# Wider steps between the blocks of the up operands, the projection weights and the out-projection weights in SBUF

## The chip, the cores and the metric

The kernel runs on one core of one Trainium2 chip. The metric is the device time of one execution in microseconds (us), lower being better. The kernel before takes 1240.32 us, the median of three runs (1239.75 to 1241.23).

## The reference

One decoder layer on x of 1024 tokens by 1024 features, in float32:

```
h    = rms_norm(x, norm1_w)
proj = h @ w_in                        # 1024 x 3592
A    = differential attention of 4 heads over proj's first 1536 columns
B    = gated DeltaNet of 4 heads: causal conv + SiLU of the next 1536 columns (q, k, v),
       chunked delta rule; gated by silu(z), z and two small gates being the last 520 columns
x    = x + concat(A, B) @ w_out        # 1024 x 1024
h    = rms_norm(x, norm2_w)
out  = x + square(relu(h @ w_up)) @ w_down   # hidden 4096
```

## The kernel before

Every large product works on float32 numbers that are split in two float32r parts. ScalarE (ACT) rounds a block to a high part, VectorE (DVE) subtracts it from the block and so writes the low part. A product then takes three matmuls for each block of 128 of the summed dimension: high by high, high by low and low by high. The normed and transposed activations lie as such pairs in hH and hL: eight blocks (k) of 1024 columns for each partition, so that one block starts 4096 bytes behind the one before. Each matmul has a stationary operand of 128 columns (512 bytes a partition), loaded by an instruction of its own (PEld), and a moving operand of 256, 260 or 512 columns that streams through.

The stages, in order of time:

1. **Gates (z)**, to 58 us. `z_mm` (L370 to L381) multiplies hH and hL (stationary) by two units of 260 weight columns (moving). Each unit has eight blocks of 260 columns, laid one behind the other: 1040 bytes from block to block.
2. **DeltaNet projections (ps_dn)**, 58 to 230 us. `load_unit` (L183) fetches 256 columns of weights and rounds them in steps of two blocks (L192 on ACT, L193 on DVE); `trn` (L275) makes a block of the weights the stationary operand, and 512 columns of hH or hL the moving one. Interleaved are the transposes, convolutions and triangular inverses of the delta rule.
3. **Attention projections (ps_qk)**, 230 to 460 us. `da_units` (L1037) makes hH and hL stationary and 256 columns of weights moving (L1063 to L1065). The weights come by `Quarters.unit` (L253) and its roundings (L224, L225). An interleaving planner (`Interleave`) puts the steps of the scan over chunks, of the attention scores and of the values between the matmuls.
4. **Out-projection (ps_op)**, 460 to 620 us. `half` (L1325) has hH and hL stationary and 512 columns of w_out moving (L1332 to L1334), four blocks a unit, again from `Quarters.unit`. Attention's last scores and values and the second norm stand between them.
5. **Up**, 620 to 928 us. `prod_up` (L1503) makes 128 columns of an up operand stationary and 512 tokens of hH and hL, or of sums of them (T0 to T2), moving. An operand is a high and a low tile `op` of four blocks by 256 columns, rounded by `split` (L1425, L1426) from `operand` (L1604), or by `rounded` and `rest` (L1630, L1634). The tiles rotate through five buffers. The first 96 of these matmuls (`up_first`) take other tiles.
6. **Down**, from 928 us. `down` (L1789) takes both operands from views of hH and hL.

In the built program the starts of hH, hL, both wH, both wL, T0 to T2 and all five op buffers have the same remainder, 320, when divided by 512. Blocks of the weights with 256 columns start 1024 bytes apart, those with 512 columns 2048, and those of op 1024: the remainder stays the same from block to block. In the gates alone it moves by 16 bytes a block.

TensorE's order in stages 3 to 6 is written out (`manual_schedule`); a scheduler orders what the source leaves open. The functions that the change touches:

Of the kernel before, what the change touches and what calls it, by code (L numbers as in the profile page):

```python
# [10 lines left out]
F32R = mybir.dt.float32r  # L11
# [7 lines left out]
P = 128  # L19
SEQ = 1024  # L20
DM = 1024
KB = DM // P
# [6 lines left out]
UC = 260  # L29
# [91 lines left out]
def tile_hymba_layer(  # L121
# [28 lines left out]
    def laid(tag):  # L150
        if tag in ahead:
            return ahead.pop(tag)
        pool, shape, dt, bufs = FORMS[tag]
        return pool.tile(shape, dt, tag=tag, name=tag, bufs=bufs)

    def staged(tag):
        turns[tag] += 1
        return laid(f"{tag}{1 - turns[tag] % 2}")
# [21 lines left out]
    hH = hpool.tile([P, KB, SEQ], F32R, name="hH")  # L180
    hL = hpool.tile([P, KB, SEQ], F32R, name="hL")

    def load_unit(src, k0=0, nk=KB):  # L183
        width = src.shape[-1]
        wh, wl = staged("wH"), staged("wL")
        wh = wh[:, :nk * width].rearrange("p (k c) -> p k c", k=nk)
        wl = wl[:, :nk * width].rearrange("p (k c) -> p k c", k=nk)
        st = 2 * UC // width
        for k in range(0, nk, st):
            raw = laid("wraw")[:, :st * width].rearrange("p (k c) -> p k c", k=st)  # L190
            nc.sync.dma_start(raw, src[:, k0 + k:k0 + k + st, :])
            S.copy(wh[:, k:k + st, :], raw)  # L192
            V.tensor_tensor(wl[:, k:k + st, :], raw, wh[:, k:k + st, :].bitcast(F32), ALU.subtract)  # L193
        return wh, wl

    class Quarters:
# [55 lines left out]

        def unit(self, width, nk):  # L253
            wh, wl = staged("wH"), staged("wL")
            wh = wh[:, :nk * width].rearrange("p (k c) -> p k c", k=nk)
            wl = wl[:, :nk * width].rearrange("p (k c) -> p k c", k=nk)
            st = nk // 4
            self.begin([(wh[:, k:k + st, :], wl[:, k:k + st, :]) for k in range(0, nk, st)])
            return (wh, wl), [0.0] * 4
# [406 lines left out]
    def dn_proj(kind):  # L666
        for pr in range(2):
            with tc.issue_after(x_last.ins) if kind == 1 and pr == 0 else ExitStack():
                w = load_unit(w_units[6 + 2 * kind + pr])
            for hl in range(2):  # L670
                h = 2 * pr + hl
                u = 4 * kind + h
                cp = cps[hl]
                for hf in range(2):
                    ps = pj.tile([P, 512], F32, tag="pj", name="ps_dn")
                    trn(ps, w, hl * P, hf)
                    b = 512 * hf
                    S.copy(cp[:, 3 + b:3 + b + 512], ps)  # L678
                    y = ta("cy", 2)
                    S.activation(y, cp[:, 3 + b:3 + b + 512], AF.Copy, scale=pv[:, 36 + u:37 + u])  # L680
                    for wi in (2, 1, 0):
                        V.scalar_tensor_tensor(y, cp[:, wi + b:wi + b + 512], pv[:, 12 * wi + u:12 * wi + u + 1],  # L682
                                               y, ALU.mult, ALU.add)
                    if kind == 1:
                        th = ta("cth", 2)
                        S.activation(th, y, AF.Tanh, scale=0.5)
                        yield h, hf, y, th
                    else:
                        o = ta("cth" if hf else "k2", 2)
                        S.activation(o, y, AF.Silu)  # L690
                        yield h, hf, o
# [35 lines left out]
    for h in range(HEADS):  # L727
        for hf in range(2):
            rh, rl = ta("rrh", 1, F32R), ta("rrl", 1, F32R)
            for t, col in ((rh, ggh), (rl, ggl)):  # L730
                for c in range(4):
                    i = cidx(h, 4 * hf + c)
# [26 lines left out]
    for h, hf, y, th in skew(dn_proj(1)):  # L759
# [6 lines left out]
        for c in range(4):  # L766
            i = cidx(h, 4 * hf + c)
# [9 lines left out]
        for c in range(4):  # L777
            i = cidx(h, 4 * hf + c)
# [50 lines left out]
    for h, hf, q2 in skew(dn_proj(0)):  # L829
# [6 lines left out]
        for c in range(4):  # L836
            i = cidx(h, 4 * hf + c)
# [3 lines left out]
        for c in range(4):  # L841
            i = cidx(h, 4 * hf + c)
# [194 lines left out]
    def da_units():  # L1037
        todo = [(g, kind) for g in range(2) for kind in (1, 0, 2)]

        w = load_unit(w_units[2 * todo[0][1] + todo[0][0]]), unit_time()  # L1040
        for g, kind in todo[1:]:
            quarters.plan(w_units[2 * kind + g])
# [380 lines left out]
    def split(dst, src):  # L1423

        S.copy(dst[0], src)  # L1425
        V.tensor_tensor(dst[1], src, dst[0].bitcast(F32), ALU.subtract)  # L1426
# [148 lines left out]
    op_ = octx.enter_context(tc.tile_pool(name="op", bufs=1, **right))  # L1575
# [16 lines left out]
    w = {0: dict(zip("abcd", raws))}  # L1592
# [9 lines left out]
                w.setdefault(g, {})[n] = t  # L1602

    def operand(src):  # L1604
        o = [op_.tile([P, 4, 256], F32R, tag="op", name="op", bufs=5) for _ in range(2)]
        split(o, src)
        return o

# [15 lines left out]
    early = {}  # L1624
# [3 lines left out]
        V.tensor_tensor(w[g][dst], w[g][l], w[g][r], op)  # L1628

    def rounded(g, i):  # L1630
        early[g, i] = [op_.tile([P, 4, 256], F32R, tag="op", name="op", bufs=5) for _ in range(2)]
        S.copy(early[g, i][0], w[g][CH[i]])

    def rest(g, i):  # L1634
# [9 lines left out]
    held(2, [0, 1])  # L1644
    combine(0, 5)
    rounded(0, 5)
    held(0, [2, 3])
    held(1, [2])
    rest(0, 5)
    held(1, [3])  # L1650
    read_first()
    combine(0, 6)
    rounded(0, 6)
    combine(0, 3)
    held(2, [2, 3])
# [4 lines left out]
    def product(g, i):  # L1660
# [10 lines left out]
        else:  # L1671
            bank = [x[:, p] for p in range(2)]
        o = early.pop((g, i), None) or (operand(w[g][CH[i]]) if g > 1 or i > 2 else None)
        for p in range(2) if o else ():
            for _ in prod_up(bank[p], o, p, H_OPS[i], i in (1, 2, 5) or (i == 4 and last), i in (2, 3, 4)):
# [45 lines left out]
    def step(g, i):  # L1721
        puts.append([])
        product(g, i)
        flush(2)

    rounded(0, 3)
    step(0, 5)
    rest(0, 3)
# [181 lines left out]
```

## Time and profile before

| | us |
|---|---|
| Median of the runs shown | 1240.32 |
| Span of the profiled execution | 1237.3 |
| Difference, outside the span | 3.0 |
| PE busy | 1222.9 |
| PEld busy | 1053.6 |
| DVE busy | 824.9 |
| ACT busy | 618.7 |

The profile has one row for each matmul, with its start and its own duration. The duration covers the way through the array too, so that consecutive matmuls overlap in the rows: a row of 0.39 us may be followed by the next after 0.23 us. What fills the time is the **pitch**, the distance from one start to the next. It is read from the timeline (first and last start of a run of matmuls, divided by the number of steps); the durations in the grouped rows move with it.

### The profile page before, as it was taken

What the parts mean: (1) busy time and instruction counts of PE and PEld (TensorE: products, weight loads), DVE (VectorE), ACT (ScalarE), POOL (GpSimd) and SP (SyncE); (2) the same over time, 40 slices, a digit from 0 to 9 for tenths busy, and PEclk for the clock granted to TensorE, in tenths of its full rate; (3) what the DMA queues carried; (4) which work ended last, traced back from release to release, by engine and by line L of the source; (5) the groups of instructions that cost most, each with busy time, mean ns of one, the idle gap of its engine ahead of it and who ended that gap; (6) DMA issues with size and microseconds to landing.
All of it is one profiled execution on the core that took longest, in us unless ns stands there. A gap on an engine that the chain in (4) does not pass through costs nothing.

```text
span 1237.3 us, 18898 instructions
## 1 busy us (share of the span) xinstructions
PE 1222.9 (99%) x6887; PEld 1053.6 (85%) x6887; DVE 824.9 (67%) x1458; ACT 618.7 (50%) x1249; POOL 154.6 (12%) x215
## 2 busy tenths in 40 slices
PE   9999999999999999999999999999999999999998
PEld 8978888899998998888888888888888888888886
DVE  6868796566647656777689555566569755777543
ACT  6587554244445555566667444544564333333330
POOL 2411110034335421111200000000000000000000
PEclk9999999999999999999999999999999999999999
DMA  9344653179648755223346534444469655432301
GB/s 350 104 112 119 167 158 108 56 238 270 212 141 256 219 163 151 82 72 115 125 147 223 189 122 157 180 156 153 167 234 376 237 179 186 166 102 102 137 34 68
DMA packets 143301, 202.12 MB, mean 163 GB/s; under 512 B 20920, under 2 KB 98280, under 8 KB 143208
## 3 DMA queue, kind: packets, MB, share of 16 engines
q1 hardware_dynamic: 138584, 187.28, 46.6%
q0 software_dynamic: 4480, 13.64, 2.9%
q8 instruction: 54, 0.88, 0.3%
q14 instruction: 39, 0.32, 0.1%
q10 hardware_dynamic: 144, 0.00, 0.0%
HBM read 135.86 MB, written 65.01 MB: 162 GB/s over the span
## 4 chain that ended last, share of the span: by engine, by line
PE 93%; DMA 2%; DVE 2%; ACT 1%; issue 1%; POOL 1%; DVEq 0%; SPq 0%; ACTq 0%; POOLq 0%
PE X L1509 5%; PE X L1507 5%; PE X L1508 5%; PE X L1806 4%; PE X L1805 4%; PE X L1807 4%; PE ps_dn L265 3%; PE ps_dn L267 3%; PE ps_dn L266 3%; PE ps_qk L1063 3%; PE ps_qk L1064 3%; PE ps_qk L1065 3%; PE Y L1507 3%; PE Y L1509 2%; PE Y L1508 2%; PE ps_op L1332 2%
## 5 line engine op out<-in xcount | busy, mean ns | idle before, releaser
L1425 ACT CAST hH<-ur 128x1024 fp32r<-128x1024 f32 x56 | 58.9, 1051 | 173.2 <-PE Y L1806 89.4
L1426 DVE TENSOR_TENSOR hL<-ur,hH 128x1024 fp32r<-128x1024 f32 x56 | 68.4, 1223 | 79.8 <-ACT hH L1425 79.7
L1063 PE MATMUL ps_qk<-wH,hH 128*128 128x256 f32 x384 | 114.6, 299 | 0.1
L1065 PE MATMUL ps_qk<-wH,hL 128*128 128x256 f32 x384 | 108.6, 283 | 0.0
L1064 PE MATMUL ps_qk<-wL,hH 128*128 128x256 f32 x384 | 108.4, 282 | 0.0
L1426 DVE TENSOR_TENSOR op<-raw,op 128x1024 fp32r<-128x1024 f32 x48 | 58.7, 1223 | 74.2 <-PE X L1508 41.2
L1805 PE MATMUL X<-hH 128*128 128x512 f32 x224 | 87.1, 389 | 0.0
L1806 PE MATMUL X<-hL,hH 128*128 128x512 f32 x224 | 87.1, 389 | 0.0
L1807 PE MATMUL X<-hH,hL 128*128 128x512 f32 x224 | 87.1, 389 | 0.0
L265 PE MATMUL ps_dn<-hH,wH 128*128 128x512 f32 x192 | 76.3, 397 | 0.2 <-ACT cp L678 0.2
L267 PE MATMUL ps_dn<-hH,wL 128*128 128x512 f32 x192 | 75.8, 396 | 0.0
L266 PE MATMUL ps_dn<-hL,wH 128*128 128x512 f32 x192 | 75.8, 395 | 0.0
L1063 PEld LDWEIGHTS ps_qk<-wH,hH 128*128 128x128 f32 x384 | 73.4, 191 | 0.3 <-ACT qn L1082 0.2
L1064 PEld LDWEIGHTS ps_qk<-wL,hH 128*128 128x128 f32 x384 | 73.4, 191 | 0.0
L1065 PEld LDWEIGHTS ps_qk<-wH,hL 128*128 128x128 f32 x384 | 73.1, 190 | 0.0
L1426 DVE TENSOR_TENSOR hL<-dw,hH 128x1024 fp32r<-128x1024 f32 x56 | 68.2, 1218 | 0.9 <-ACT hH L1425 0.9
L1425 ACT CAST op<-raw 128x1024 fp32r<-128x1024 f32 x48 | 50.4, 1052 | 35.7 <-PE Y L1509 19.9
L1425 ACT CAST hH<-dw 128x1024 fp32r<-128x1024 f32 x56 | 58.7, 1048 | 10.8 <-DMA dw<-in_w_down_dram 5.1
L1198 ACT ACTIVATE pexp<-ps_sc,mx 128x128 f32<-128x128 f32 (+7 forms) x64 | 47.5, 743 | 30.4 <-DVE mx L1194 30.0
L682 DVE SCALAR_TENSOR_TENSOR cy<-cp,pv,cy 128x512 f32<-128x512 f32 x72 | 53.7, 746 | 8.3 <-ACT cy L680 7.5
L1332 PE MATMUL ps_op<-wH,hH 128*128 128x512 f32 x128 | 54.7, 427 | 0.0
L1194 DVE TENSOR_REDUCE mx<-ps_sc 128x1 f32<-128x128 f32 (+7 forms) x64 | 47.4, 752 | 10.6 <-PE ps_sc L1192 10.0
(368 smaller groups left out, 3452.8 us busy)
## 6 DMA issues: line engine op xcount, KB each, us to landing
ur<-ud SPq DMA_DIRECT2D x28, 1024.0 KB, 4.9
raw<-in_w_up_dram SPq DMA_DIRECT2D x32, 512.0 KB, 3.9
dw<-in_w_down_dram SPq DMA_DIRECT2D x32, 512.0 KB, 7.2
wraw<-in_w_units_dram SPq DMA_DIRECT2D x48, 256.0 KB, 3.8
qk_d<-qa POOLq DMA_DIRECT2D x32, 256.0 KB, 3.9
ud<-ua SPq DMA_DIRECT2D x16, 512.0 KB, 4.5
ud<-s SPq DMA_DIRECT2D x16, 512.0 KB, 2.7
pka<-park_d SPq DMA_DIRECT2D x32, 192.0 KB, 4.2
```

The source lines that it names most:

```text
L265: T.matmul(ps, lh(k), rh(k), start=(k == 0), stop=False)
L266: T.matmul(ps, lh(k), rl(k), start=False, stop=False)
L267: T.matmul(ps, ll(k), rh(k), start=False, stop=(k == n - 1))
L1063: T.matmul(ps[:, :256], hH[:, k, sl], wh[:, k, :], start=(k == 0), stop=False)
L1064: T.matmul(ps[:, :256], hH[:, k, sl], wl[:, k, :], start=False, stop=False)
L1065: T.matmul(ps[:, :256], hL[:, k, sl], wh[:, k, :], start=False, stop=(k == KB - 1))
L1425: S.copy(dst[0], src)
L1426: V.tensor_tensor(dst[1], src, dst[0].bitcast(F32), ALU.subtract)
L1507: T.matmul(ps, op[0][:, k, cs], h[0][:, k, :], start=start and k == 0, stop=False, skip_group_check=True)
L1805: T.matmul(bank[t], v[0][:, j, sl], v[2][:, j], start=s0, stop=False, skip_group_check=True)
L1806: T.matmul(bank[t], v[0][:, j, sl], v[3][:, j], start=False, stop=False, skip_group_check=True)
L1807: T.matmul(bank[t], v[1][:, j, sl], v[2][:, j], start=False, stop=s1, skip_group_check=True)
```

## The change

A helper `spread` lays the blocks of a weight unit over the whole tile of 8 x 260 columns, whatever their width. Eight blocks of 256 columns then start 1040 bytes apart in place of 1024, four blocks of 512 columns 2080 bytes apart in place of 2048. The op tiles get four blocks of 264 columns, of which 256 are used: 1056 bytes apart in place of 1024. The weight tiles keep their size and place; an op buffer grows by 128 bytes, and the five op buffers start at remainders 64, 192, 192, 320 and 448 of 512.

```diff
+    def spread(w, width, nk):
+        return w[:, :KB * UC].rearrange("p (k c) -> p k c", k=nk)[:, :, 0:width]
...
     def load_unit(src, k0=0, nk=KB):
         width = src.shape[-1]
         wh, wl = staged("wH"), staged("wL")
-        wh = wh[:, :nk * width].rearrange("p (k c) -> p k c", k=nk)
-        wl = wl[:, :nk * width].rearrange("p (k c) -> p k c", k=nk)
+        wh, wl = [spread(w, width, nk) for w in (wh, wl)]
...
         def unit(self, width, nk):
             wh, wl = staged("wH"), staged("wL")
-            wh = wh[:, :nk * width].rearrange("p (k c) -> p k c", k=nk)
-            wl = wl[:, :nk * width].rearrange("p (k c) -> p k c", k=nk)
+            wh, wl = [spread(w, width, nk) for w in (wh, wl)]
...
     def operand(src):
-        o = [op_.tile([P, 4, 256], F32R, tag="op", name="op", bufs=5) for _ in range(2)]
+        o = [op_.tile([P, 4, 264], F32R, tag="op", name="op", bufs=5)[:, :, 0:256] for _ in range(2)]
...
     def rounded(g, i):
-        early[g, i] = [op_.tile([P, 4, 256], F32R, tag="op", name="op", bufs=5) for _ in range(2)]
+        early[g, i] = [op_.tile([P, 4, 264], F32R, tag="op", name="op", bufs=5)[:, :, 0:256] for _ in range(2)]
```

## The prediction

> **What bounds the kernel now.** I read the page's busy times and its chain first, then the busy times by stage, then the groups of matmuls, then the starts of single matmuls.
>
> ```profile
> PE 1222.9 (99%) x6887; PEld 1053.6 (85%) x6887; DVE 824.9 (67%) x1458; ACT 618.7 (50%) x1249; POOL 154.6 (12%) x215
> ...
> PE 93%; DMA 2%; DVE 2%; ACT 1%; issue 1%; POOL 1%; DVEq 0%; SPq 0%; ACTq 0%; POOLq 0%
> ```
>
> ```profile
> 58.17:230.30 172.13, 171.46 (x943) 143.53 (x942) 132.39 (x325) 102.52 (x309) 22.01 (x25) 1.00 0.47 129
> 230.30:460.50 230.20, 225.28 (x1928) 218.34 (x1927) 139.56 (x385) 112.53 (x328) 87.39 (x117) 1.00 0.67 204
> 460.50:620.30 159.80, 158.98 (x937) 133.60 (x935) 114.73 (x252) 97.38 (x257) 25.86 (x38) 1.00 0.39 112
> 620.30:927.60 307.30, 307.30 (x1367) 254.18 (x1365) 198.00 (x197) 162.95 (x176) 1.40 (x2) 1.00 0.49 172
> ```
>
> TensorE is busy for 1222.9 of 1237.3 us and holds 93% of the chain. The four stages whose operands the change moves (columns: window, its length, then PE, PEld, DVE, ACT, POOL, granted clock) leave it idle for 6.4 us in all, at clock 1.00. So the kernel is TensorE's stream of matmuls, and a change shows in the time only if it moves the pitch at which they start.
>
> ```profile
> L1063 PE MATMUL ps_qk<-wH,hH 128*128 128x256 f32 x384 | 114.6, 299 | 0.1
> L1065 PE MATMUL ps_qk<-wH,hL 128*128 128x256 f32 x384 | 108.6, 283 | 0.0
> L1064 PE MATMUL ps_qk<-wL,hH 128*128 128x256 f32 x384 | 108.4, 282 | 0.0
> ...
> L267 PE MATMUL ps_dn<-hH,wL 128*128 128x512 f32 x192 | 75.8, 396 | 0.0
> L266 PE MATMUL ps_dn<-hL,wH 128*128 128x512 f32 x192 | 75.8, 395 | 0.0
> ...
> L1334 PE MATMUL ps_op<-wH,hL 128*128 128x512 f32 x128 | 50.4, 393 | 0.0
> L1333 PE MATMUL ps_op<-wL,hH 128*128 128x512 f32 x128 | 50.0, 391 | 0.0
> L1507 PE MATMUL Y<-hH,op 128*128 128x512 f32 x128 | 49.9, 390 | 0.0
> L1509 PE MATMUL Y<-hH,op 128*128 128x512 f32 x128 | 49.8, 389 | 0.0
> L1508 PE MATMUL Y<-hL,op 128*128 128x512 f32 x128 | 49.8, 389 | 0.0
> ```
>
> ```profile
> 620.30:927.60 307.30, 174.78 (x448) 84.06 (x448) 1.00 0.49 172
> ```
>
> The groups give the counts, three lines of equal count a product: 3 x 384 = 1152 matmuls of 256 columns in ps_qk, 3 x 192 = 576 of 512 columns in ps_dn, 3 x 128 = 384 in ps_op. The last row is L1507 alone in the up stage's window: 3 x 448 = 1344 matmuls, of which 96 read the tiles of `up_first` and 1248 read op. Together 3360 matmuls have one operand moved. Their pitch stands in the timeline (start, duration):
>
> ```profile
> 891.19 0.39 PE L1508 MATMUL X<-T1l,op 128*128 128x512 f32 x1
> ...
> 902.97 0.39 PE L1509 MATMUL X<-T2h,op 128*128 128x512 f32 x1
> ```
>
> ```profile
> 340.26 0.28 PE L1065 MATMUL ps_qk<-wH,hL 128*128 128x256 f32 x1
> ...
> 342.78 0.28 PE L1065 MATMUL ps_qk<-wH,hL 128*128 128x256 f32 x1
> ```
>
> ```profile
> 63.58 0.40 PE L266 MATMUL ps_dn<-hL,wH 128*128 128x512 f32 x1
> ...
> 65.67 0.39 PE L267 MATMUL ps_dn<-hH,wL 128*128 128x512 f32 x1
> ...
> 67.48 0.39 PE L265 MATMUL ps_dn<-hH,wH 128*128 128x512 f32 x1
> ```
>
> ```profile
> 32.11 0.28 PE L378 MATMUL ps_z<-wH,hH 128*128 128x260 f32 x1
> ...
> 33.54 0.29 PE L378 MATMUL ps_z<-wH,hH 128*128 128x260 f32 x1
> 33.67 0.28 PE L379 MATMUL ps_z<-wL,hH 128*128 128x260 f32 x1
> ...
> 34.97 0.28 PE L378 MATMUL ps_z<-wH,hH 128*128 128x260 f32 x1
> ```
>
> Up: 52 steps in 11.78 us, 226.5 ns each. ps_qk: 21 steps in 2.52 us, 120.0 ns. Between the two widths a column costs (226.5 - 120.0) / 256 = 0.416 ns, so 512 columns are 213 ns and 256 are 106.5, and every matmul pays some 13.5 ns more, whatever its width. I call this pitch **settled**: all operands have remainder 320 there. ps_dn shows the other state. Behind a break, 9 steps take 2.09 us, 232.2 ns each; the next 8 take 1.81 us, 226.3. So a disturbed stream of 512 columns runs 5.7 ns a matmul slower and needs some nine matmuls to settle. The gates show what a step of 16 bytes a block does: 24 matmuls in 2.86 us are 119.2 ns each for 260 columns, but single steps differ (0.13 us behind 33.54, 0.12 on the mean), and the stream doesn't settle into one pitch. The place of a block matters, then, by some ns.
>
> **The change part by part.** No instruction is added, removed or reordered on any engine, no DMA changes, and one wait of an up matmul on DVE falls away, in a stage where PE never idles: nothing. What moves is addresses.
>
> *Roundings.* ACT and DVE now write two pieces of 256 columns with a gap, or four, where they wrote 512 or 1024 in one run.
>
> ```profile
> L1425 ACT CAST hH<-dw 128x1024 fp32r<-128x1024 f32 x56 | 58.7, 1048 | 10.8 <-DMA dw<-in_w_down_dram 5.1 <-issue 3.7 <-PE Y L1807 2.0
> ...
> L1425 ACT CAST op<-raw 128x1024 fp32r<-128x1024 f32 x48 | 50.4, 1052 | 35.7 <-PE Y L1509 19.9 <-PE X L1509 8.0 <-PE Z L1509 6.5
> ```
>
> The first of these writes two pieces of 512 that lie 4096 bytes apart, the second one run of 1024: 1048 against 1052 ns, so a gap costs nothing. Were it 5%, it would hide under PE: in the up stage ACT is busy for 163 us and DVE for 198 of 307.
>
> *ps_qk, moving operand by 16 bytes a block.* This is the gates' layout, with the same tiles, 4 columns narrower. If those columns cost 0.416 ns each, its pitch is 119.2 - 1.7 = 117.5: -2.5 ns. If they hide, it is 119.2: -0.8 ns. I take the middle, -1.65 ns: 1152 x -1.65 = **-1.9 us** (-2.9 to -0.9).
>
> *Up, stationary operand by 32 bytes a block.* No row has 512 columns at moving remainders for long. Bounds: the gates' -2.5 ns from below (-3.1 us), the 5.7 ns of the disturbed run from above (+7.1 us). A new remainder after every third matmul looks to me like the break, repeated before the nine matmuls are over; the nearest row is the out-projection's, where other work breaks the stream every few matmuls: L1334 lasts 393 ns and L1333 391 against 389 to 390 for the up stage. I take +4 ns, the upper row against 389: 1248 x 4 = **+5.0 us**.
>
> *ps_dn, stationary operand by 16 bytes.* Its means of 395 and 396 hold breaks and unsettled runs; I estimate that half of its matmuls run settled now and would lose the same 4 ns: 288 x 4 = **+1.2 us** (576 x -2.5 = -1.4 to 288 x 5.7 = +1.6).
>
> *ps_op, moving operand by 32 bytes.* It hardly settles now, so there is little to lose: **0** (384 x -2.5 = -1.0, to +1.0 if 2.5 ns are lost).
>
> Sum: -1.9 + 5.0 + 1.2 + 0 = +4.3 us. The profiled execution has 1237.3 us, and the median stands 3.0 us above its span: 1237.3 + 4.3 + 3.0 = **1244.6 us**. The bounds add up to -8.4 and +8.8: 1231.9 and 1249.1.
>
> The Trainium skill (TensorE: Matmul & The Clock Gate, "Back-to-back issue gap") puts the gap of warm matmuls at N / 2.4 + 2.5 ns, 215.8 for 512 columns. The trace is 10.7 ns above that; if the change brought all 3360 there, my estimate by that page would be some 36 us of gain, and no row of these stages comes near it.
>
> **The rivals.**
>
> *The settled pitch is itself the expensive one (faster).* Equal remainders might make the load of one operand meet the stream of the other in every matmul, and the 13.5 ns would be that price. The gates speak for it: their 119.2 less 108.2 for 260 columns leaves 11.0, not 13.5. Against it: ps_dn runs slower, not faster, while it is out of step. If the gates' 2.5 ns hold at both widths, all 3360 gain: -8.4 us, 1231.9. It decides from the point where the 2208 matmuls of 512 columns lose under 1.9 us / 2208 = 0.9 ns each.
>
> *Addresses don't matter (no change).* The gates' wobble could come from 260 columns not being a multiple of 16, and ps_dn's slow run from the break alone; then nothing moves, and the median stays at 1240.3. For it: the up stage mixes op with hH and with T0 to T2, and its groups show 389 or 390.
>
> The Trainium skill (SBUF — State Buffer, "Who interferes with whom") speaks for this rival: TensorE reads the moving operand and the weights through two independent ports and waits on no one. By it the sum is 0. The trace agrees only in part, since 226.3 and 232.2 ns stand side by side with the same operands.
>
> *The stream never settles (much slower).* All upper bounds together: 1249.1; this is the far end of the forecast, not a case of its own.
>
> **How the numbers follow.** A measurement of this kernel can tell about 0.2% from no change, 2.5 us. The forecast gets 0.48 (0.45 of it over 1242.8), the faster rival 0.30 (0.28 of it under 1237.8), no change 0.22 (0.17 within, 0.03 faster, 0.02 slower). That gives faster 0.31, within 0.22, slower 0.47. The range runs from 1233 to 1249: it leaves out the last us of the faster rival and what lies beyond the upper bounds, some 0.15 together. The forecast's own range is 1241 to 1249.
>
> **What would show it.** Right: the up stage lasts about 5 us longer than 307.3, its groups (L1507 to L1509) rise from 389 to about 393 ns, single steps there vary where they were alike, and ps_qk's L1064 falls from 282 to about 280. Wrong: up groups at or under 389, which leaves the faster rival if L1064 falls too, and no change if nothing moves; or a stage in which ACT or DVE now ends PE's wait.

## The result and the profile after

The changed kernel takes 1245.96 us, the median of four runs (1245.26 to 1248.48), against 1240.03 us for four runs of the kernel before on the same chip: a ratio of 1.0053, interval 1.0037 to 1.0069. It is 5.9 us slower. The profiled execution of the changed kernel has 1245.26 us and a span of 1243.6 us, 6.3 more than before. Two lines were added in the first part of the file, so that the up stage is now L1509 to L1511, ps_qk L1065 to L1067, ps_op L1334 to L1336 and ps_dn L267 to L269.

The page of the changed kernel, busy times and chain:

```profile
PE 1231.0 (99%) x6887; PEld 1052.9 (85%) x6887; DVE 824.5 (66%) x1458; ACT 618.8 (50%) x1249; POOL 155.2 (12%) x215
...
PE 92%; DMA 3%; DVE 2%; ACT 1%; issue 1%; POOL 0%; SPq 0%; DVEq 0%; ACTq 0%; POOLq 0%
```

PE has 8.1 us more of busy time over the same 6887 matmuls; ACT, DVE, POOL and the weight loads have what they had. In the stages that the change touches, the waits that are new or longer come to 0.4 us (0.3 of ps_o on ACT, 0.1 of ps_dn on ACT), and one of 1.3 us on a DMA is gone. The same view by stage, cut at the first matmul of ps_dn, ps_qk, ps_op, up and down (window, length, PE, PEld, DVE, ACT, POOL, clock, DMA):

```profile
58.85:232.43 173.58, 173.32 (x943) 143.75 (x942) 131.69 (x325) 102.75 (x310) 22.05 (x25) 1.00 0.46 128
232.43:459.97 227.54, 224.00 (x1932) 217.19 (x1931) 139.76 (x385) 113.15 (x330) 87.67 (x118) 1.00 0.67 207
459.97:620.09 160.12, 159.17 (x931) 133.12 (x931) 114.91 (x252) 96.77 (x256) 25.80 (x38) 1.00 0.37 112
620.09:933.90 313.81, 313.81 (x1367) 254.61 (x1366) 197.85 (x197) 164.01 (x177) 1.28 (x2) 1.00 0.47 168
933.90:1243.60 309.70, 304.80 (x1345) 252.15 (x1343) 198.05 (x180) 106.79 (x107) 0.00 (x0) 1.00 0.44 159
```

The same cuts of the kernel before:

```profile
58.17:230.33 172.16, 171.49 (x943) 143.53 (x942) 132.39 (x325) 102.54 (x310) 22.01 (x25) 1.00 0.47 129
230.33:461.11 230.78, 225.86 (x1933) 218.85 (x1931) 139.56 (x385) 113.11 (x330) 87.59 (x118) 1.00 0.67 204
461.11:620.29 159.18, 158.36 (x931) 133.08 (x931) 114.72 (x252) 96.76 (x256) 25.66 (x37) 1.00 0.38 112
620.29:927.68 307.39, 307.39 (x1368) 254.23 (x1366) 198.01 (x197) 163.04 (x176) 1.41 (x2) 1.00 0.49 172
927.68:1237.30 309.62, 304.80 (x1345) 252.06 (x1343) 197.97 (x180) 107.93 (x108) 0.00 (x0) 1.00 0.44 159
```

Stage by stage: DeltaNet projections +1.4 us, attention projections -3.2, out-projection +0.9, up +6.4, down 0.1. The first stage is 0.7 longer, but no operand of it moved, and in the profiles below its end wanders from 58.1 to 60.7 us. In the up stage PE never idles in either kernel, so all of the 6.4 us is pitch. The groups of matmuls of the changed kernel (busy us, mean ns of one):

```profile
L1065 PE MATMUL ps_qk<-wH,hH 128*128 128x256 f32 x384 | 114.1, 297 | 0.1
L1067 PE MATMUL ps_qk<-wH,hL 128*128 128x256 f32 x384 | 107.8, 281 | 0.0
L1066 PE MATMUL ps_qk<-wL,hH 128*128 128x256 f32 x384 | 107.6, 280 | 0.0
...
L268 PE MATMUL ps_dn<-hL,wH 128*128 128x512 f32 x192 | 76.5, 398 | 0.0
L269 PE MATMUL ps_dn<-hH,wL 128*128 128x512 f32 x192 | 76.2, 398 | 0.0
...
L1335 PE MATMUL ps_op<-wL,hH 128*128 128x512 f32 x128 | 50.5, 394 | 0.0
L1509 PE MATMUL Y<-hH,op 128*128 128x512 f32 x128 | 50.4, 394 | 0.0
L1511 PE MATMUL Y<-hH,op 128*128 128x512 f32 x128 | 50.4, 394 | 0.0
```

Every group of 512 columns whose operands moved rose (up 389 to 394, ps_dn 396 to 398, L1335 391 to 394), and ps_qk fell by 2 ns. The timeline shows it in single starts (`...` marks rows left out). In the up stage of the changed kernel the next start comes after 0.23 or 0.24 us, where 226.5 ns mean 0.22 and 0.23:

```profile
896.56 0.39 PE L1510 MATMUL X<-T1l,op 128*128 128x512 f32 x1
896.79 0.39 PE L1511 MATMUL X<-T1h,op 128*128 128x512 f32 x1
897.02 0.40 PE L1509 MATMUL X<-T1h,op 128*128 128x512 f32 x1
897.26 0.40 PE L1510 MATMUL X<-T1l,op 128*128 128x512 f32 x1
...
899.12 0.40 PE L1509 MATMUL X<-T1h,op 128*128 128x512 f32 x1
```

These are 11 steps in 2.56 us, 232.7 ns each, where they had 226.5. In ps_qk 16 steps of the changed kernel take 1.87 us, 116.9 ns, where 21 settled ones before took 120.0 each:

```profile
340.06 0.28 PE L1066 MATMUL ps_qk<-wL,hH 128*128 128x256 f32 x1
...
341.93 0.28 PE L1067 MATMUL ps_qk<-wH,hL 128*128 128x256 f32 x1
```

Over all starts that follow one another without other work between them, the mean pitch in ns is as follows. The step right behind other work, some 200 ns in ps_qk, is not counted.

| stage (columns) | before | after |
|---|---|---|
| gates (260) | 119.6 | 119.6 |
| ps_dn (512) | 228.6 | 232.3 |
| ps_qk (256) | 119.5 | 117.8 |
| ps_op (512) | 229.8 | 232.5 |
| up (512) | 226.8 | 231.8 |
| down (512) | 226.7 | 226.7 |

The change does two opposite things: it slows every stream of 512 columns that it touches and quickens the one of 256. In ps_dn 341 of 507 such steps took at most 228 ns before and 43 after; in ps_op it was 127 of 278, then 22.

### The profile page after: what moved, and what is told of

The parts are those of the page before. It is cut to its first block, busy times and chain, and to the rows that moved or that the text cites. A ratio compares the mean times of both kernels' runs of the same rounds, so it can differ in the third digit from the quotient of the medians.

```text
span 1243.6 us, 18899 instructions
## 1 busy us (share of the span) xinstructions
PE 1231.0 (99%) x6887; PEld 1052.9 (85%) x6887; DVE 824.5 (66%) x1458; ACT 618.8 (50%) x1249; POOL 155.2 (12%) x215
## 4 chain that ended last, share of the span: by engine, by line
PE 92%; DMA 3%; DVE 2%; ACT 1%; issue 1%; POOL 0%; SPq 0%; DVEq 0%; ACTq 0%; POOLq 0%
PE X L1510 5%; PE X L1509 5%; PE X L1511 5%; PE X L1809 4%; PE X L1808 4%; PE X L1807 4%; PE ps_dn L267 3%; PE ps_dn L268 3%; PE ps_dn L269 3%; PE ps_qk L1065 3%; PE ps_qk L1066 3%; PE ps_qk L1067 3%; PE Y L1510 3%; PE Y L1509 3%; PE Y L1511 3%; PE ps_op L1334 2%
## 5 line engine op out<-in xcount | busy, mean ns | idle before, releaser
L1065 PE MATMUL ps_qk<-wH,hH 128*128 128x256 f32 x384 | 114.1, 297 | 0.1
L1067 PE MATMUL ps_qk<-wH,hL 128*128 128x256 f32 x384 | 107.8, 281 | 0.0
L267 PE MATMUL ps_dn<-hH,wH 128*128 128x512 f32 x192 | 77.0, 401 | 0.3 <-ACT cp L680 0.3
L269 PE MATMUL ps_dn<-hH,wL 128*128 128x512 f32 x192 | 76.2, 398 | 0.0
L1065 PEld LDWEIGHTS ps_qk<-wH,hH 128*128 128x128 f32 x384 | 72.5, 189 | 0.3 <-ACT qn L1084 0.2
L1067 PEld LDWEIGHTS ps_qk<-wH,hL 128*128 128x128 f32 x384 | 72.3, 188 | 0.0
L1427 ACT CAST op<-raw 128x1024 fp32r<-128x1024 f32 x48 | 50.3, 1048 | 38.0 <-PE Y L1511 21.0
L1427 ACT CAST hH<-dw 128x1024 fp32r<-128x1024 f32 x56 | 58.7, 1048 | 10.1 <-DMA dw<-in_w_down_dram 4.4
L1334 PE MATMUL ps_op<-wH,hH 128*128 128x512 f32 x128 | 54.9, 429 | 0.0
```

Of the source, the lines that this page charges most:

```text
L267: T.matmul(ps, lh(k), rh(k), start=(k == 0), stop=False)
L269: T.matmul(ps, ll(k), rh(k), start=False, stop=(k == n - 1))
L1065: T.matmul(ps[:, :256], hH[:, k, sl], wh[:, k, :], start=(k == 0), stop=False)
L1067: T.matmul(ps[:, :256], hL[:, k, sl], wh[:, k, :], start=False, stop=(k == KB - 1))
```

## The experiments

The theory at the start was that of the prediction: a stream of 512 columns settles only while the remainders of its operands stay the same from block to block, and a step between blocks unsettles it. The rivals: it is not the step but how the two operands lie to each other that costs; 16 bytes are good and 32 bad, whatever the width; the parts act on each other. Times of one kernel stand against runs of the kernel before on the same chip.

### Streams of matmuls alone, first set (mb1)

```diff
+            for r in range(reps):
+                for k in range(4):
+                    if mode in "ub":
+                        a = 256 * k + (step * k + const) // 4 + 128 * (r % 2)
+                        e = 1024 * k + (step * k // 4 if mode == "b" else 0)
+                        seq += [(w[i][:, a:a + 128], h[j][:, e:e + n]) for i, j in ((0, 0), (0, 1), (1, 0))]
...
```

Here a is where the stationary operand starts and e where the moving one does, counted in elements of 4 bytes; `step` and `const` are in bytes.

> Computes nothing of the layer: it loads x, copies it to the output and runs 34 unbroken streams of float32r matmuls on rounded copies of x, each stream into its own PSUM tile, read by its pitch (start to start). Streams of 144 matmuls with 512 columns: stationary operand stepping 0 to 512 bytes extra a block (us0 to us512), stationary operand at a constant offset of 16 to 256 bytes (uc16 to uc256), moving operand stepping (os0 to os64); streams of 48 (256 or 260 columns): moving operand stepping (qs, zs) or at a constant offset (qc). Theory (a 512-column stream settles only while the operands' remainders stay the same from block to block; a step unsettles it): us0, os0 and every uc at 226.6 ns, us16 to us64 and os16 to os64 at about 232; qs16 117.8 against qs0 120.0, every qc 120.0. Where the address counts only by its remainder of 128 or 512 bytes, us128 to us512 or us512 alone fall back to 226.6. Rival (what counts is how the two operands of one matmul lie to each other): uc32 is as slow as us32, about 232, and qc16 as fast as qs16, 118. Rival (16 bytes are good and 32 bad, whatever the width): us16 and os16 at about 224, qs32 above 120.

The stretches below are the second halves of nine streams, from the start of one matmul to the start of the last: 71 steps for those of 512 columns, 95 for those of 256. Columns: window, length, PE busy with its count, clock, DMA.

```profile
120.84:137.37 16.53, 16.53 (x72) 1.00 0.00 0
221.79:238.26 16.47, 16.47 (x73) 1.00 0.00 1
255.08:271.17 16.09, 16.09 (x72) 1.00 0.00 1
355.14:371.71 16.57, 16.57 (x72) 1.00 0.00 0
591.25:607.35 16.10, 16.10 (x73) 1.00 0.00 0
691.01:707.58 16.57, 16.57 (x72) 1.00 0.00 1
753.14:764.54 11.40, 11.40 (x98) 1.00 0.00 0
913.29:924.37 11.08, 11.08 (x97) 1.00 0.01 1
1010.49:1026.94 16.45, 16.45 (x73) 1.00 0.00 1
```

In this order they are us32 (232.8 ns), us128 (232.0), us256 (226.6), uc32 (233.4), uc256 (226.8), os32 (233.4), qs0 (120.0), qc32 (116.6) and ub32 (231.7). By the starts of all streams, second half, in ns:

| offset in bytes | 0 | 16 | 32 | 48 | 64 | 128 | 256 | 512 |
|---|---|---|---|---|---|---|---|---|
| stationary steps, 512 columns | 226.7 | 232.2 | 232.8 | 232.5 | 231.7 | 231.9 | 226.7 | 226.7 |
| stationary constant, 512 | | 233.3 | 233.4 | 233.3 | 233.4 | 232.3 | 226.7 | |
| moving steps, 512 | 226.7 | 231.1 | 233.4 | | 231.7 | | | |
| moving steps, 256 | 120.0 | 117.6 | 118.3 | 117.9 | 118.3 | 118.9 | | |
| moving constant, 256 | | 116.7 | 116.7 | | 117.8 | | | |

The theory falls: a constant offset costs as much as a step, or more. What counts is the distance between the operands, and only its remainder of 256 bytes; steps of 256 and 512 cost nothing. Stationary or moving, 16 or 32 bytes makes little difference, and constant offsets of 80, 96 and 112 bytes, not in the table, have 232.0, 234.3 and 233.3. The width decides the sign here: with a distance, 512 columns lose 4 to 8 ns and 256 columns gain 1 to 3. In ub32 both operands step together, so that each matmul's own two operands never part, and it is still slow. So a matmul's own distance is not all: its distance to its neighbours' operands counts too, or the step of the place does.

### The up operands alone (up_only)

```diff
-        o = [op_.tile([P, 4, 256], F32R, tag="op", name="op", bufs=5) for _ in range(2)]
+        o = [op_.tile([P, 4, 264], F32R, tag="op", name="op", bufs=5)[:, :, 0:256] for _ in range(2)]
```

> Only the op tiles get blocks of 264 columns; all weights lie as before. Theory: the up stage alone brings its 1248 x 5.0 = 6.2 us: 1246.3 us, ratio 1.005, with pitch 231.8 there and 226.8 everywhere else where 512 columns settle. Rival (the up stage also suffers from what the other parts change): under 3 us, ratio under 1.0025.

Measured: 1246.19 us against 1239.38, ratio 1.0061, interval 1.0048 to 1.0075. Its stages ps_dn, ps_qk, ps_op and up:

```profile
58.43:230.69 172.26, 171.46 (x943) 143.51 (x942) 132.32 (x325) 102.66 (x310) 22.03 (x25) 1.00 0.46 129
230.69:460.26 229.57, 225.38 (x1933) 218.72 (x1931) 139.43 (x385) 113.15 (x330) 87.59 (x118) 1.00 0.66 205
460.26:619.60 159.34, 158.40 (x932) 133.09 (x931) 114.70 (x252) 96.74 (x256) 25.65 (x38) 1.00 0.37 112
619.60:933.37 313.77, 313.77 (x1367) 254.59 (x1366) 197.89 (x197) 164.03 (x177) 1.41 (x2) 1.00 0.47 168
```

The up stage has the 313.8 us of the changed kernel, and the two others of 512 columns their length of before. The op tiles alone make the whole loss of that stage. The attention stage, unchanged here, is 1.2 us shorter than in the profile of before. By the starts 0.95 of it falls between 296 and 315 us, around a wait for a DMA that the experiment on the attention weights describes.

### The op buffers 32 bytes lower, no step (up_base)

```diff
-    octx.enter_context(tc.tile_pool(name="pad", bufs=1, **right)).tile([P, 40], F32, name="pad")
+    octx.enter_context(tc.tile_pool(name="pad", bufs=1, **right)).tile([P, 48], F32, name="pad")
```

> The op tiles keep their packed blocks, but all five buffers lie 32 bytes lower (a pad of 48 columns in place of 40), so that the stationary operand has remainder 288 of 512 against 320 of the moving one, the same in every block. Theory (a changing remainder unsettles the stream, a constant offset doesn't): pitch 226.8 and the time before, 1240 us, ratio 1.000. Rival (the offset between the two operands is what costs): pitch about 231.8 and 1246 us, ratio 1.005. A third way: the offset makes it settle lower, as in the gates, by 1.7 ns: 1238 us, ratio 0.998.

Measured: 1247.43 us, ratio 1.0068, interval 1.0056 to 1.0081. The groups of its up stage and the stage:

```profile
L1507 PE MATMUL Y<-hH,op 128*128 128x512 f32 x128 | 50.7, 396 | 0.1
L1509 PE MATMUL Y<-hH,op 128*128 128x512 f32 x128 | 50.6, 395 | 0.0
L1508 PE MATMUL Y<-hL,op 128*128 128x512 f32 x128 | 50.6, 395 | 0.0
```

```profile
620.74:936.48 315.74, 315.66 (x1368) 253.92 (x1366) 197.71 (x197) 164.34 (x177) 1.41 (x2) 1.00 0.47 167
```

The blocks are packed and every one has the same remainder, and still the stage is 8.4 us longer than before, 2 more than with the step. In the kernel too the distance costs, without any change from block to block.

### The op buffers 256 bytes lower (up_base256)

```diff
-    octx.enter_context(tc.tile_pool(name="pad", bufs=1, **right)).tile([P, 40], F32, name="pad")
+    octx.enter_context(tc.tile_pool(name="pad", bufs=1, **right)).tile([P, 104], F32, name="pad")
```

> The five op buffers lie 256 bytes lower than before (remainder 64 of 512 against 320 of the moving operands), blocks packed. Theory (only the remainder of 256 counts): the up stage as before, pitch 226.8, 1239.5 us, ratio 1.000. Rival (any offset of 512 or less costs, or the place of the buffers as such): as with 32 bytes, 1247 us, ratio 1.006.

Measured: 1240.36 us against 1239.56, ratio 1.0008, interval 1.0000 to 1.0017. Pitch 226.8 ns, and the stage:

```profile
621.51:929.64 308.13, 307.55 (x1367) 254.31 (x1366) 197.85 (x197) 162.93 (x176) 1.40 (x2) 1.00 0.49 171
```

```profile
L1507 PE MATMUL Y<-hH,op 128*128 128x512 f32 x128 | 49.9, 390 | 0.6 <-DVE ua L1547 0.6
```

The pitch is that of before; the 0.7 us more is mostly the idle 0.6 us ahead of L1507, behind a DVE operation. A distance of 256 bytes costs what none does.

### DeltaNet projections and out-projection alone (dn_op)

```diff
+    def load_unit(src, k0=0, nk=KB, span=KB * UC):
...
+        wh = wh[:, :span].rearrange("p (k c) -> p k c", k=nk)[:, :, 0:width]
...
         def unit(self, width, nk):
...
+            span = nk * width if nk == KB else KB * UC
...
+        w = load_unit(w_units[2 * todo[0][1] + todo[0][0]], span=KB * 256), unit_time()
```

The last line is the first attention unit, which stays packed.

> Only the units of the DeltaNet projections and of the out-projection are spread; the attention units and the op tiles lie as before. Theory (every stream of 512 columns loses once its operands' remainders differ): ps_dn from 228.6 to 232.3 and ps_op from 229.8 to 232.4 ns as in the changed kernel, its stages 1.4 and 0.9 us longer: 1242.4 us, ratio 1.0019. Rival (the breaks by other work hide it): under 0.8 us, ratio under 1.0007.

Measured: 1242.78 us against 1239.44, ratio 1.0024, interval 1.0014 to 1.0034. Its pitches are 232.3 and 232.4 ns. The stages ps_dn and ps_op:

```profile
60.70:234.69 173.99, 173.41 (x944) 143.77 (x942) 132.58 (x325) 102.81 (x310) 22.03 (x25) 1.00 0.45 127
...
465.00:625.10 160.10, 159.15 (x932) 133.15 (x931) 114.84 (x252) 96.64 (x256) 25.76 (x38) 1.00 0.37 112
```

They are 1.8 and 0.9 us longer than in the kernel before. The breaks by other work do not hide the loss.

### Attention projections alone (qk_only)

```diff
+            span = KB * UC if nk == KB else nk * width
-            wh = wh[:, :nk * width].rearrange("p (k c) -> p k c", k=nk)
+            wh = wh[:, :span].rearrange("p (k c) -> p k c", k=nk)[:, :, 0:width]
```

> Only the eight-block units of the attention projections are spread (16 bytes a block); all other operands lie as before. Theory (256 columns gain, 512 columns lose): ps_qk's pitch falls from 119.5 to 117.8 as in the changed kernel, 1152 x -1.66 = -1.9 us, with the gaps between them -1.9 to -3.2; the DeltaNet projections, the out-projection and the up stage keep their length: 1237 us, ratio 0.997 to 0.9985. Rival (the changed kernel's gain in this stage is only work shifted from the stage before it): 1240, ratio 1.000.

Measured: 1238.94 us, ratio 0.9993, interval 0.9985 to 1.0002: under what was expected, and not told apart from no change. The first of the six units, which comes by `load_unit`, stayed packed, so that only 960 matmuls moved: 960 x -1.66 = -1.6 us. The mean pitch did fall, to 118.0. The waits of PE between 230 and 462 us (total, times, longest), first in the kernel before, then here, show what lies over it:

```profile
PE ps_o L966 <- DMA pkb<-park_d: 1.3, 1, 1.3
```

```profile
PE ps_o L967 <- DMA pkb<-park_d: 1.6, 1, 1.6
```

Near 296 and 307 us the scan waits for pkb, which a DMA reads back. This wait differs from run to run: the longest is 1.3 us before, 0.8 in up_only (whose stage is the same program), 1.6 here, and the changed kernel's profile has none. By the starts, the profile here loses 3 us near 296 against before and gets some 2 back by 311. The wait itself is only about half of these 3 us. Behind it the granted clock falls: the clock is the last figure but two of this row (window, length, PE, PEld, DVE, ACT, POOL, clock, DMA).

```profile
299.40:302.90 3.50, 3.50 (x20) 3.50 (x19) 2.84 (x8) 1.16 (x3) 0.60 (x1) 0.55 0.69 215
```

In it 14 matmuls of ps_qk start 213 to 218 ns apart, which is 1.3 us more than at 118 ns; the mean of 118.0 leaves them out. No profile of another version of the kernel shows a lowered clock in this stage, so this one shows less of the gain than the pitch is worth. Whether the other runs of this version had such a stretch isn't shown. In the changed kernel, about 1.3 of the 3.2 us that the stage gained is the missing wait, and not the pitch.

### Attention weights at a constant distance (qk_const, qk_const16, qk_const64)

If the distance counts, all attention weights can be moved at once, with the 512-column streams left alone. The packed blocks start 32, 16 or 64 bytes later in their tile (`off` is 8, 4 or 16 elements of 4 bytes):

```diff
+            off = 8 if nk == KB else 0
-            wh = wh[:, :nk * width].rearrange("p (k c) -> p k c", k=nk)
+            wh = wh[:, off:off + nk * width].rearrange("p (k c) -> p k c", k=nk)
...
-        w = load_unit(w_units[2 * todo[0][1] + todo[0][0]]), unit_time()
+        w = load_unit(w_units[2 * todo[0][1] + todo[0][0]], off=8), unit_time()
```

> The eight-block units of the attention projections are packed as before but start 32 bytes later in their tile, so that all 1152 matmuls of 256 columns have their operands 32 bytes off each other; the 512-column streams keep equal remainders. Theory: pitch 116.7 in place of 119.5 in ps_qk, 1152 x -2.8 = -3.2 us, 1236 us, ratio 0.9975. Rival (the attention stage is held by its waits, above all the read-back of pkb by DMA, so that a shorter pitch is taken back): pitch 116.7 but under 1 us of gain, ratio above 0.999.

> As the kernel with the attention weights 32 bytes later, with 16 bytes in place of 32. Theory (the stream alone says what the stage does: 113.3 ns at 16 bytes, 117.8 at 32, 120.0 at 0): ps_qk at about 113.5, 1152 x -6.0 = -6.9 us, 1232.5 us, ratio 0.9945. Rival (in the kernel other work breaks the stream every few matmuls, so that no pattern lasts): pitch near the 116.9 of 32 bytes, 1238.5, ratio 0.998 to 0.999.

> As the kernels with the attention weights 16 and 32 bytes later, with 64 bytes. Theory (in the kernel every break starts the stream at another phase, so that any unequal remainder gives about the same mean): ps_qk at 116.5 to 118, 1152 x -2 to -3 = -2 to -3.5 us, 1236.5 to 1238, ratio 0.9972 to 0.9985. Rival (the offset sets the pitch): as in the short streams of the grid, 113.4 ns, 1233 us, ratio 0.9945.

| | us | kernel before | ratio, interval | pitch of ps_qk, ns |
|---|---|---|---|---|
| 16 bytes | 1237.18 | 1240.09 | 0.9974 (0.9962 to 0.9985) | 117.0 |
| 32 bytes | 1238.93 | 1239.56 | 0.9983 (0.9974 to 0.9992) | 116.9 |
| 64 bytes | 1238.30 | 1239.44 | 0.9991 (0.9980 to 1.0001) | 117.6 |

The ratio is worked out over all runs of both kernels and is not the quotient of the two medians. The groups of ps_qk at 16 bytes, and the stage there:

```profile
L1064 PE MATMUL ps_qk<-wH,hH 128*128 128x256 f32 x384 | 113.5, 296 | 0.1
L1066 PE MATMUL ps_qk<-wH,hL 128*128 128x256 f32 x384 | 107.3, 279 | 0.0
L1065 PE MATMUL ps_qk<-wL,hH 128*128 128x256 f32 x384 | 107.2, 279 | 0.0
```

```profile
231.66:459.82 228.16, 223.32 (x1932) 216.31 (x1931) 139.66 (x385) 113.04 (x330) 88.22 (x118) 1.00 0.67 206
```

The version at 16 bytes is faster than both kernels: 0.15 to 0.38% under before. At 64 bytes the interval takes in 1, so that its gain is not told apart from none. By the pitch the three should gain 2.8, 2.9 and 2.2 us (1152 times the fall from 119.5); by the ratios they gain 3.2, 2.1 and 1.1, each within its interval. The 113.3 ns that a stream alone has at 16 bytes did not come, and the three offsets lie within 0.7 ns of each other.

### Streams alone, second set: distance or place, own operands or neighbours (mb2)

```diff
+                a, e = at(i)
+                a += 1024 * (i // 3 % 4) + 128 * (i // 12 % 4)
+                e += 1024 * (i // 3 % 8)
+                T.matmul(ps[:, :n], w[i % 3 == 2][:, a:a + 128], h[i % 3 == 1][:, e:e + n],
```

`at` gives the two offsets of matmul i, another function for each stream.

> Computes nothing of the layer: copies x to the output and runs 38 unbroken streams of float32r matmuls on rounded copies of x. Theory now (what counts is the distance between the two operands of neighbouring matmuls, taken by its remainder of 256 bytes): both operands 32 bytes further (b32_512) settles at 226.7 ns like al512, while s32 and m32 stay at 233.3. In same_512 every matmul has both operands at one remainder but its neighbour at another, in next_512 the operands of one matmul differ and the moving operand agrees with the stationary one of the next: if a load meets the stream of the matmul before it, next_512 is at 226.7 and same_512 at 233; if it meets its own, the other way round. Rival (the remainder itself counts, not the distance): b32_512 at 233. With one matmul in 2, 3, 6, 12, 24, 48 off by 32 bytes (ev2 to ev48), settling over some nine matmuls gives 232 up to 12 and falls only behind that; without such a memory ev12 would be at 227.2. Widths: if the cost of distant remainders grows with the columns (10 ns at 256, 20 at 512) and that of equal ones is 13.3 ns whatever the width, the two lines cross near 340 columns: s32 is faster than al at 128 to 320 and slower at 384 to 480; s32_384 at 175 ns against al384 at 173.3.

The timeline of the second half of b32_512, both operands 32 bytes further (start, duration), first and last of 74 matmuls:

```profile
153.97 0.39 PE L73 MATMUL b<-hL,wH 128*128 128x512 f32 x1
...
170.52 0.40 PE L73 MATMUL b<-hH,wL 128*128 128x512 f32 x1
```

That is 73 steps in 16.55 us, 226.7 ns each; with one of the operands off it is 233.3 and 233.4 (s32_512 and m32_512, second halves like all that follow). So the place itself doesn't count, the distance does. same_512 has 231.6 and next_512 230.0: neither settles, and which of the two distances weighs more is not told by this. With one matmul in 48, 24, 12, 6 and 3 off by 32 bytes, the pitch is 227.1, 227.5, 228.3, 230.0 and 233.4; less 226.7 and times the period that is 19 to 20 ns for each matmul off, with no longer memory. With one in 2 it is 235.0, more than with all of them off. Even 4 and 8 bytes cost: 232.4 and 230.7. My nine matmuls of settling are wrong for this kind of disturbance: at one in 6, two steps later the pitch is back. Widths, equal and 32 bytes off, ns:

| columns | 128 | 192 | 256 | 320 | 384 | 448 | 480 | 512 |
|---|---|---|---|---|---|---|---|---|
| equal | 111.7 | 111.6 | 120.0 | 146.7 | 173.3 | 202.7 | 216.7 | 226.7 |
| 32 bytes off | 111.7 | 111.7 | 118.3 | 146.6 | 173.3 | 204.5 | 213.3 | 233.3 |

The two lines that I expected to cross near 340 columns don't exist: 320 and 384 show no difference, and 480 columns gain. At 256 columns the size of the distance matters as well: with the moving operand 16, 32, 64, 96 and 128 bytes off the pitch is 113.3, 117.8, 117.8, 120.0 and 118.7, so that 96 bytes gain nothing.

### Streams alone, a grid of offsets (mb3)

```diff
-                a, e = at(i)
+                a, e = (a1 if i % 3 == 2 else a0) // 4, (b1 if i % 3 == 1 else b0) // 4
...
+CONFIGS = [(512, 24, a0, a1, 0, 0) for a0 in range(0, 256, 16) for a1 in range(0, 256, 16)]
+CONFIGS += [(256, 30, 0, 0, b0, b1) for b0 in range(0, 128, 16) for b1 in range(0, 128, 16)]
```

> Computes nothing of the layer: copies x to the output and runs 362 short streams of float32r matmuls, 24 of 512 columns or 30 of 256, in the kernel's order (high by high, high by low, low by high) over a grid of byte offsets of the four operands in steps of 16 bytes: 16 x 16 offsets of the two stationary operands at 512 columns, 8 x 8 of the two moving ones at 256. The pitch of each is read behind the first twelve matmuls. Theory (equal remainders of 256 bytes are the best place for 512 columns): no place of the grid is under 226.6 ns, the place (0, 0) is the only one at it, most lie at 228 to 235. Rival (equal remainders are only one good place among others): some places come under 222 ns. At 256 columns: both moving operands 16 bytes off give 113.4 ns as in the stream before, equal ones 120.0, and places with the low part elsewhere lie between 113 and 120.

No place of the 16 x 16 grid at 512 columns is under 226.6 ns. Five places are at it: high and low stationary part at (0, 16), (0, 144), (0, 240), (240, 16) and (240, 144) bytes; (0, 0) itself was the first stream, with TensorE still at 427 ns a matmul in its first half, and had not settled (229.9 over its last seven steps). The rest lie between 227.9 and 235.9. So the equal place isn't the only good one, but none is better. At 256 columns the 64 places lie between 113.4 and 120.4, with equal ones at 120.0; (16, 16), which had 113.3 in the set before, has 116.5 here. The same offsets gave another pitch, then. Not every distance gains at 256 columns: both moving operands 96 bytes off have 119.7, and 4 and 20 bytes, tried behind the grid, have 123.2 and 122.3.

### Streams alone, eight starts (mb4)

```diff
-            for _ in range(2):
+            for _ in range(t):
                 T.transpose(ps[:, 0:P], ident, ident)
```

t runs from 1 to 8.

> Computes nothing of the layer: copies x to the output and runs ten offsets (512 columns with the stationary operand 0, 16, 32, 128, 256 bytes off, 256 columns with the moving operand 0, 16, 32, 64, 112 bytes off), each in eight streams of 48 matmuls that differ only in the number of transposes ahead of them, 1 to 8; the pitch is read over the last 30. Theory (equal remainders lead into one pitch from any start; other distances keep the phase that the break left): offsets 0 and 256 give 226.7 ns (512 columns) and 120.0 (256) in all eight, the others spread over some ns: 231 to 235, and 113 to 120. Rival (each offset has its own pitch, and the streams before differed by something else): all eight agree at every offset, within 0.3 ns.

| offset | the eight streams, ns |
|---|---|
| 512 columns, 0 and 256 bytes | 226.6 to 226.7 in all (the first, at the start, 227.0) |
| 512, 16 bytes | 233.3 in six, 226.7 in two |
| 512, 32 bytes | 233.3 in all |
| 512, 128 bytes | 232.2 to 233.3 |
| 256, 0 bytes | 120.0 in all |
| 256, 16 bytes | 113.3, four times 118.7, 118.6, twice 116.7 |
| 256, 32 bytes | 116.5 to 117.8 |
| 256, 64 bytes | 117.8 in seven, 113.3 in one |
| 256, 112 bytes | 113.3 in all |

Equal remainders give one pitch from each of these starts. Others depend on more than the offset. The number of transposes alone doesn't fix it: 16 bytes at 256 columns behind two of them has 118.7 here, 113.3 in the second set and 116.5 in the grid. That the break ahead sets the phase of the stream would explain this, and also why 16 bytes gives 117.0 in the kernel, where other work breaks the stream every few matmuls; it is argued, not shown. The offset 112 gave 113.3 eight times; it was not tried in the kernel, and stays open.

## Why the prediction was right, and where its reason was not

The time came out as forecast in direction and nearly in size: +4.3 us predicted, +5.9 between the medians. That the sum is so near is in part luck: up and ps_op cost 2.3 us more than forecast in the profile, and a wait for a DMA that was missing there took 1.3 us back.

- **Bound.** Right. PE's busy time and the span moved together (+8.1 and +6.3), and in the stages touched no wait of PE on ACT or DVE grew by more than 0.3 us. The roundings of op take 1048 ns (1052 before): no cost, as said.
- **ps_qk, -1.65 ns each.** It measured 119.5 to 117.8, and that the digit agrees is luck: -1.65 was the middle between two cases. The streams alone decide for the first, in which the four columns cost: stepping by 16 bytes, 260 columns have 119.2 ns and 256 have 117.6. The kernel's mean before was also 119.5 and not the settled 120.0. The stage gained 3.2 and not 1.9 us, since the profile after had no wait for pkb. That the gates' layout gains at 256 columns held; the step is not needed for it: constant distances gain more (117.0 at 16 bytes).
- **Up, +4 ns each, +5.0 us.** Right in sign, under in size: 6.42 us / 1248 = 5.1 ns, within the upper bound of 5.7. The step of the reasoning that failed is that "a new remainder after every third matmul" is the break repeated. up_base has no new remainder at all and loses 8.4 us in the stage; mb2 prices a single matmul 32 bytes off at some 20 ns, without nine matmuls of settling. It is the distance of the operands by its remainder of 256 bytes. In the changed kernel the op buffers start at 64 or 192 of 256 and step by 32, the moving operands at 64, so that of eight kinds of block one is at no distance.
- **ps_dn, +1.2 us.** Right in sign and nearly in size, +1.4 in the changed kernel and +1.8 in dn_op, by the same wrong reason as up. The share that ran settled was under-estimated: 341 of 507 steps, not half.
- **ps_op, 0.** Wrong, at its upper bound: +0.9 us in both kernels. "It hardly settles now" overlooked that its mean was 229.8 ns: 127 of 278 steps ran at 228 ns or less. After the change 22 do, and the mean is 232.5.
- **The faster rival** (equal remainders are the dear place) is true at 256 columns against most offsets tried and false at 512: no offset of the grid brought a 512-column stream under 226.6 ns. That is why the change has both signs in it.
- **Addresses don't matter** is refuted by up_base and up_base256: the same program, buffers 32 or 256 bytes lower, 1247.4 and 1240.4 us. The Trainium skill (SBUF — State Buffer, "Who interferes with whom") has PE read moving operand and weights through two ports and wait on no one. The traces show no wait of the up stage's matmuls on another engine either, and still the pitch differs by 6.7 ns with the distance of the two operands; the measurement decides.
- **The Trainium skill's gap** (TensorE: Matmul & The Clock Gate, "Back-to-back issue gap"), N / 2.4 + 2.5 ns: by it an estimate of 215.8 for 512 columns and 109.2 for 256. The section gives this formula for an isolated matmul, which the prediction didn't say, and about 131 ns at 512 columns for a stream of loads and matmuls. The best streams here, with a load for each matmul, have 226.6 and 113.3; no offset tried gave less, and the measurement decides.

What stays open: why the sign turns with the width and why a few distances cost nothing at 512 columns (16 bytes in two of eight starts) or gain nothing at 256 (96 bytes), whether a load meets its own matmul's stream or its neighbour's, and what fixes the pitch at a distance other than zero. The profile has no counter of SBUF accesses that would show a collision; that there is one is only argued.

## What to carry to other kernels

Where TensorE's stream is the bound, as here, the place of the operands in SBUF is part of the schedule: take the start of each stationary and moving operand by its remainder of 256 bytes, keep them equal for float32r streams of 512 columns, and try a constant distance for streams of 256. Of those, 16 and 32 bytes gained in this kernel; in the streams alone 96 bytes gained nothing and 4 and 20 were dearer. Move the whole tile rather than its blocks, one stream at a time. Read the pitch from starts: the mean durations move with it by only 2 to 5 ns, a short stretch at a lower clock can cover that as in qk_only, and the busy share doesn't show it. The pad of up_base, 32 bytes more, cost 8 us of 1240 without a single wait of TensorE in the up stage.

## What the runs showed of the hardware that I had not expected

- Matmuls of 128 and 192 columns follow one another in 111.7 ns, nearly as long as 256 columns at their best (113.3): in these streams, with a load for each matmul, a float32r matmul under 256 columns gains almost nothing.
- 260 columns at equal remainders have 119.5 ns in the first set and 118.7 in the second, less than 256 columns (120.0 in both).
- With 0.417 ns a column (226.7 less 120.0, over 256 columns), equal remainders cost the same 13.3 ns on top at 256, 320, 384 and 512 columns (120.0, 146.7, 173.3, 226.7), but 16.0 and 16.7 at 448 and 480. The prediction's "whatever its width" holds at some widths only.
- In the first of the streams alone, right behind the loads, matmuls of 512 columns come 427 ns apart for 6 to 12 steps before they come at 227.
- Behind an idle time of 1.6 us near 298 us, the profile of qk_only has granted clock 0.55 from 299.4 to 302.9 us, and matmuls of 256 columns 213 to 218 ns apart. The 1.3 us of the kernel before were followed by no such stretch.
